# Rotary embedding over eight batches: the first small store takes two rows a partition in place of one

## The chip, the core and the metric

The kernel runs on one core of a Trainium2 chip. The metric is the device time of one execution in microseconds (us). Before the change the median of 3 runs is 317.09 us (316.78 to 317.14).

## The reference

The input x has 8 batches of 2048 positions, 16 heads and 64 values, in float32. Each head is split into two halves of 32 values, and each pair of values is turned by an angle that depends on the position:

```
cos = cos[None, :, None, :].copy()
sin = sin[None, :, None, :].copy()
out1 = x1 * cos - x2 * sin
out2 = x1 * sin + x2 * cos
return np.concatenate([out1, out2], axis=-1).astype(np.float32)
```

There are three operations for each value. 67.1 MB of x are read and as much is written.

## The kernel before

**Tiling.** The 2048 positions of a batch lie on 128 partitions, so a partition holds J = 16 consecutive positions, called rows here. A row is 16 heads of 64 values: 4 KB in DRAM (float32) and 2 KB on chip (float16). One tile `xt` holds a whole batch, 32 KB a partition. A pool of NBUF = 5 tiles serves the eight batches, so batch 5 takes over the tile of batch 0, batch 6 that of batch 1, and batch 7 that of batch 2.

**Transfers.** The loads (L52) and nearly all stores (L60, L100, L130, L132) are issued by GpSimd, which lets the transfer change the type on the way: a load turns float32 into float16, and a store turns it back. Three small transfers at the start are issued by SP: the first JA = 2 rows of batch 0 in float32 (`head`, L36), and the sine and cosine tables (L44, L45). ScalarE turns these into float16 (L84, L88 to L90). SP also sends the last two rows of batch 7 out (L141), after ScalarE has turned them into float32 in `head` (L140).

**Arithmetic.** `rotate` has three VectorE instructions: x with its halves swapped times the signed sine, into a scratch tile `v` (L73), x times the cosine in place (L79), and the sum of the two, again in place (L81). Batch 0 is rotated in two parts: rows 0 and 1 first, which need only the `head` rows, and then rows 2 to 15. Batches 1 to 7 are rotated whole.

**Order.** GpSimd issues its transfers in the order in which they stand in its program, and it waits before an issue until what the transfer needs is ready. The order is this: load 0 (rows 2 to 15), load 1, the small store of batch 0's row 0 (L100), loads 2, 3 and 4, the store of batch 0's rows 1 to 15, store 1, load 5, load 6, store 2, store 3, load 7, stores 4, 5 and 6, and batch 7 in pieces of 9 rows (`gate`, L130) and 5 rows (`rest`, L132). The place of the small store is set by hand: two ordering edges without a semaphore put it behind load 1 and ahead of load 2. Load 5 waits until batch 0 is stored, load 6 until batch 1 is, and load 7 until batch 2 is. SP's last store waits for `gate` to land.

Of the kernel before, what the change touches and what calls it, by code (L numbers as in the profile page):

```python
# [1 line left out]

# [4 lines left out]


@with_exitstack  # L10
def kernel(
    ctx: ExitStack,
    tc: tile.TileContext,
    x: bass.AP,
    cos: bass.AP,
    sin: bass.AP,
    out: bass.AP,
):
    nc = tc.nc
    f16 = mybir.dt.float16  # L20
    f32 = mybir.dt.float32

    B, S, H, D = x.shape
    Dh = D // 2
    P = nc.NUM_PARTITIONS
    J = S // P
    NBUF = 5

    const_pool = ctx.enter_context(tc.tile_pool(name="rope_const", bufs=1))
    io_pool = ctx.enter_context(tc.tile_pool(name="rope_io", bufs=NBUF))  # L30
    tmp_pool = ctx.enter_context(tc.tile_pool(name="rope_tmp", bufs=1))

    JA = 2
    head = const_pool.tile([P, JA, H, D], f32)
    x0 = x[0].rearrange("(p j) h d -> p j (h d)", j=J)
    nc.sync.dma_start(  # L36
        out=head.rearrange("p j h d -> p (j h d)"),
        in_=x0[:, 0:JA, :].rearrange("p j f -> p (j f)"),
    )
    sin_f = const_pool.tile([P, J, Dh], f32)  # L40
    cos_f = const_pool.tile([P, J, Dh], f32)
    cos_h = const_pool.tile([P, J, Dh], f16)
    sin_h = const_pool.tile([P, J, D], f16)
    nc.sync.dma_start(out=sin_f, in_=sin.rearrange("(p j) d -> p j d", j=J))  # L44
    nc.sync.dma_start(out=cos_f, in_=cos.rearrange("(p j) d -> p j d", j=J))  # L45

    loads = []

    def load(b):
        xt = io_pool.tile([P, J, H, D], f16)  # L50
        j0 = JA if b == 0 else 0
        dma = nc.gpsimd.dma_start(  # L52
            out=xt[:, j0:J, :, :].rearrange("p j h d -> p (j h d)"),
            in_=x[b].rearrange("(p j) h d -> p j (h d)", j=J)[:, j0:J, :].rearrange("p j f -> p (j f)"),
        )
        loads.append(dma)
        return xt

    def store(b, xt, j0=0):
        return nc.gpsimd.dma_start(  # L60
            out=out[b].rearrange("(p j) h d -> p j (h d)", j=J)[:, j0:J, :].rearrange("p j f -> p (j f)"),
            in_=xt[:, j0:J, :, :].rearrange("p j h d -> p (j h d)"),
        )

    def rotate(xt, j0, j1):
        v = tmp_pool.tile([P, J, H, D], f16)
        n = j1 - j0
        js = slice(j0, j1)
        shape = [P, n, H, 2, Dh]
        sin_b = sin_h[:, js, :].rearrange("p j (e d) -> p j e d", e=2).unsqueeze(2).to_broadcast(shape)  # L70
        cos_b = cos_h[:, js, :].unsqueeze(2).to_broadcast([P, n, 2 * H, Dh])
        xe = xt[:, js, :, :].rearrange("p j h (e d) -> p j h e d", e=2)
        nc.vector.tensor_mul(  # L73
            out=v[:, js, :, :].rearrange("p j h (e d) -> p j h e d", e=2),
            in0=xe[:, :, :, ::-1, :],
            in1=sin_b,
        )
        xw = xt[:, js, :, :].rearrange("p j h (e d) -> p j (h e) d", d=Dh)
        nc.vector.tensor_mul(out=xw, in0=xw, in1=cos_b)  # L79
        xa = xt[:, js, :, :].rearrange("p j h d -> p (j h d)")  # L80
        nc.vector.tensor_add(out=xa, in0=xa, in1=v[:, js, :, :].rearrange("p j h d -> p (j h d)"))  # L81

    tiles = [load(b) for b in range(2)]
    nc.scalar.copy(  # L84
        out=tiles[0][:, 0:JA, :, :].rearrange("p j h d -> p (j h d)"),
        in_=head.rearrange("p j h d -> p (j h d)"),
    )
    nc.scalar.copy(out=sin_h[:, :, Dh:D], in_=sin_f)  # L88
    nc.scalar.mul(out=sin_h[:, :, 0:Dh], in_=sin_f, mul=-1.0)  # L89
    nc.scalar.copy(out=cos_h, in_=cos_f)  # L90
    rotate(tiles[0], 0, JA)
    def part(b, j0, j1):
        return (
            out[b].rearrange("(p j) h d -> p j (h d)", j=J)[:, j0:j1, :].rearrange("p j f -> p (j f)"),
            tiles[b][:, j0:j1, :, :].rearrange("p j h d -> p (j h d)"),
        )

    def store_rows(b, j0, j1):
        dst, src = part(b, j0, j1)
        return nc.gpsimd.dma_start(out=dst, in_=src)  # L100

    first = store_rows(0, 0, 1)
    tc.add_manual_dep(
        first.ins,
        loads[1].ins.name,
        mybir.DependencyInfo(mybir.DependencyClass.NoSync, mybir.DependencyReason.DATA),
        reason="order of the ring",
    )
    tiles += [load(b) for b in range(2, NBUF)]
    tc.add_manual_dep(  # L110
        loads[2].ins,
        first.ins.name,
        mybir.DependencyInfo(mybir.DependencyClass.NoSync, mybir.DependencyReason.DATA),
        reason="order of the ring",
    )
    for b in range(B):
        rotate(tiles[b], JA if b == 0 else 0, J)
        if b < B - 1:
            st = store(b, tiles[b], 1 if b == 0 else 0)
            if b == 0:  # L120
                tc.add_manual_dep(
                    st.ins,
                    first.ins.name,
                    mybir.DependencyInfo(mybir.DependencyClass.NoSync, mybir.DependencyReason.DATA),
                    reason="order of the ring",
                )
        if b + NBUF < B:
            tiles.append(load(b + NBUF))
    dst, src = part(B - 1, 0, 9)
    gate = nc.gpsimd.dma_start(out=dst, in_=src)  # L130
    dst, src = part(B - 1, 9, J - JA)
    rest = nc.gpsimd.dma_start(out=dst, in_=src)  # L132
    tc.add_manual_dep(
        rest.ins,
        gate.ins.name,
        mybir.DependencyInfo(mybir.DependencyClass.NoSync, mybir.DependencyReason.DATA),
        reason="order of the ring",
    )
    dst, src = part(B - 1, J - JA, J)
    nc.scalar.copy(out=head.rearrange("p j h d -> p (j h d)"), in_=src)  # L140
    end = nc.sync.dma_start(out=dst, in_=head.rearrange("p j h d -> p (j h d)"))  # L141
    tc.add_manual_dep(
        end.ins,
        gate.ins.name,
        mybir.DependencyInfo(mybir.DependencyClass.Sync, mybir.DependencyReason.DATA),
        reason="the last rows go out behind this part",
    )


# [1 line left out]
_INS = ['x', 'cos', 'sin']  # L151
_OUTS = [((8, 2048, 16, 64), 'float32')]


# [23 lines left out]
```

## Time and profile before

| What | Value |
|---|---|
| Median of 3 runs | 317.09 us (316.78 to 317.14) |
| The profiled execution's own time | 316.67 us |
| Its span (first to last instruction) | 314.9 us |
| VectorE (DVE) busy | 209.1 us, 66% of the span, 27 instructions |
| ScalarE (ACT) busy | 6.8 us, 2% |
| GpSimd (POOL) busy | 9.9 us, 3% |
| TensorE | not used |
| Bytes moved by GpSimd's queue (q0) | 99.09 MB in 2592 packets, counted at the destination |
| Bytes moved by SP's queue (q1) | 2.62 MB in 576 packets |

The page gives busy time by engine, the span in 40 equal slices with a digit for the busy tenths, the queues of the transfers, and the costliest groups of instructions with what ended the idle time before them. Further views of the same trace list the instructions in order of time, who waited for whom, and each transfer's time from its issue to its landing. Bytes are counted where they land: a load counts its float16 bytes, a store its float32 bytes. Issuing a transfer is no busy time of the queue: what GpSimd spends on an issue (about 0.5 us) and what the transfer takes are two different numbers.

### The profile page before, as it was taken

What the parts mean: (1) busy time and instruction counts of PE and PEld (TensorE: products, weight loads), DVE (VectorE), ACT (ScalarE), POOL (GpSimd) and SP (SyncE); (2) the same over time, 40 slices, a digit from 0 to 9 for tenths busy, and PEclk for the clock granted to TensorE, in tenths of its full rate; (3) what the DMA queues carried; (4) which work ended last, traced back from release to release, by engine and by line L of the source; (5) the groups of instructions that cost most, each with busy time, mean ns of one, the idle gap of its engine ahead of it and who ended that gap; (6) DMA issues with size and microseconds to landing.
All of it is one profiled execution on the core that took longest, in us unless ns stands there. A gap on an engine that the chain in (4) does not pass through costs nothing.

```text
span 314.9 us, 122 instructions
## 1 busy us (share of the span) xinstructions
DVE 209.1 (66%) x27; ACT 6.8 (2%) x6; POOL 9.9 (3%) x22
## 2 busy tenths in 40 slices
DVE  0010699999999999999999999995009993000000
ACT  4100000000000000000000000000000002000000
POOL 1000200000000000010000000200000001000000
DMA  9899999999999899999999999999999999999997
GB/s 280 184 262 206 200 266 200 200 262 204 200 200 325 375 492 407 400 350 250 200 200 237 362 400 400 491 441 266 200 316 416 400 400 524 408 400 400 433 443 323
DMA packets 3168, 101.71 MB, mean 323 GB/s; under 512 B 352, under 2 KB 352, under 8 KB 736
## 3 DMA queue, kind: packets, MB, share of 16 engines
q0 software_dynamic: 2592, 99.09, 98.1%
q1 hardware_dynamic: 576, 2.62, 2.2%
HBM read 67.63 MB, written 67.11 MB: 428 GB/s over the span
## 4 chain that ended last, share of the span: by engine, by line
DVE 25%; DMA 22%; issue 18%; another core or an unknown queue 17%; ACT 1%; POOL 1%; SPq 0%; POOLq 0%; DVEq 0%; ACTq 0%
DMA xt<-in_x_dram 12%; DMA cos_f<-in_cos_dram 10%; DVE xt L81 8%; DVE xt L79 8%; DVE v L73 8%; ACT head L140 1%; POOL out_dram L60 0%; POOL xt L52 0%; ACT cos_h L90 0%; SPq L44 0%; SPq L36 0%; POOLq L52 0%; DVEq L73 0%; ACTq L140 0%
## 5 line engine op out<-in xcount | busy, mean ns | idle before, releaser
L73 DVE TENSOR_TENSOR v<-xt,sin_h 128x16384 f16<-128x16384 f16 (+2 forms) x9 | 69.7, 7744 | 36.0 <-DMA xt<-in_x_dram 20.0
L79 DVE TENSOR_TENSOR xt<-xt,cos_h 128x16384 f16<-128x16384 f16 (+2 forms) x9 | 69.7, 7744 | 17.4 <-ACT cos_h L90 17.2
L81 DVE TENSOR_TENSOR xt<-xt,v 128x16384 f16<-128x16384 f16 (+2 forms) x9 | 69.7, 7745 | 0.3
L52 POOL DMA_DIRECT2D xt<-in_x_dram x8 | 4.4, 556 | 110.4 <-DMA out_dram<-xt 109.6
L140 ACT CAST head<-xt 128x2048 f32<-128x2048 f16 x1 | 1.9, 1897 | 228.8 <-DVE xt L81 228.8
L60 POOL DMA_DIRECT2D out_dram<-xt x7 | 3.7, 535 | 63.6 <-DVE xt L81 63.6
L84 ACT CAST xt<-head 128x2048 f16<-128x2048 f32 x1 | 1.9, 1897 | 3.5 <-DMA head<-in_x_dram 3.5
L130 POOL DMA_DIRECT2D out_dram<-xt x1 | 0.5, 531 | 45.6 <-DVE xt L81 45.6
L100 POOL DMA_DIRECT2D out_dram<-xt x1 | 0.5, 536 | 34.5 <-DVE xt L81 34.5
L84 ACT ACT_TABLE_LOAD x1 | 1.3, 1283 | 0.7 <-PEq L162 0.7
L90 ACT CAST cos_h<-cos_f 128x512 f16<-128x512 f32 x1 | 0.6, 617 | 17.8 <-DMA cos_f<-in_cos_dram 17.8
L88 ACT CAST sin_h<-sin_f 128x512 f16<-128x512 f32 x1 | 0.6, 617 | 7.2 <-DMA sin_f<-in_sin_dram 7.2
L89 ACT ACTIVATE sin_h<-sin_f 128x512 f16<-128x512 f32 x1 | 0.6, 624 | 0.0
L132 POOL DMA_DIRECT2D out_dram<-xt x1 | 0.5, 531 | 0.0
L162 POOL MEMSET const-float32-0.0<- 128x1 f32 x1 | 0.1, 98 | 0.2 <-issue 0.2
L162 POOL MEMSET const-bfloat16-1.0<- 128x1 bf16 x1 | 0.1, 101 | 0.0
L162 POOL MEMSET const-float32-1.0<- 128x1 f32 x1 | 0.1, 98 | 0.0
L162 POOL MEMSET const-uint8-127<- 128x1 uint8 x1 | 0.1, 98 | 0.0
## 6 DMA issues: line engine op xcount, KB each, us to landing
xt<-in_x_dram POOLq DMA_DIRECT2D x7, 4096.0 KB, 38.3
out_dram<-xt POOLq DMA_DIRECT2D x1, 7680.0 KB, 60.9
out_dram<-xt POOLq DMA_DIRECT2D x1, 4608.0 KB, 42.4
xt<-in_x_dram POOLq DMA_DIRECT2D x1, 3584.0 KB, 22.3
out_dram<-xt POOLq DMA_DIRECT2D x1, 2560.0 KB, 47.9
head<-in_x_dram SPq DMA_DIRECT2D x1, 1024.0 KB, 4.8
out_dram<-head SPq DMA_DIRECT2D x1, 1024.0 KB, 8.4
out_dram<-xt POOLq DMA_DIRECT2D x1, 512.0 KB, 7.8
```

Source lines behind the costliest of these rows:

```text
L52: dma = nc.gpsimd.dma_start(out=xt[:, j0:J, :, :].rearrange("p j h d -> p (j h d)"), in_=x[b].rearrange("(p j) h d -> p j (h d)", j=J)[:, ...
L60: return nc.gpsimd.dma_start(out=out[b].rearrange("(p j) h d -> p j (h d)", j=J)[:, j0:J, :].rearrange("p j f -> p (j f)"), in_=xt[:, j0:J ...
L73: nc.vector.tensor_mul(out=v[:, js, :, :].rearrange("p j h (e d) -> p j h e d", e=2), in0=xe[:, :, :, ::-1, :], in1=sin_b,)
L79: nc.vector.tensor_mul(out=xw, in0=xw, in1=cos_b)
L81: nc.vector.tensor_add(out=xa, in0=xa, in1=v[:, js, :, :].rearrange("p j h d -> p (j h d)"))
L84: nc.scalar.copy(out=tiles[0][:, 0:JA, :, :].rearrange("p j h d -> p (j h d)"), in_=head.rearrange("p j h d -> p (j h d)"),)
L88: nc.scalar.copy(out=sin_h[:, :, Dh:D], in_=sin_f)
L89: nc.scalar.mul(out=sin_h[:, :, 0:Dh], in_=sin_f, mul=-1.0)
L90: nc.scalar.copy(out=cos_h, in_=cos_f)
L100: return nc.gpsimd.dma_start(out=dst, in_=src)
L130: gate = nc.gpsimd.dma_start(out=dst, in_=src)
L140: nc.scalar.copy(out=head.rearrange("p j h d -> p (j h d)"), in_=src)
```

## The change

The small store of batch 0 covers rows 0 and 1 (8 KB a partition) in place of row 0 alone (4 KB). The store of the rest of batch 0 covers rows 2 to 15 in place of 1 to 15. The order of the transfers is now written as a list (`plan`): "L" is a load, "R" a rotation, "S" a store, each with its batch and its rows. Each transfer that GpSimd issues has an ordering edge without a semaphore to the one before it, where there were four such edges at single places before. The branch "L4" is used by no entry of the list. The core of the diff:

```diff
-    first = store_rows(0, 0, 1)
-    tc.add_manual_dep(
-        first.ins,
-        loads[1].ins.name,
-        mybir.DependencyInfo(mybir.DependencyClass.NoSync, mybir.DependencyReason.DATA),
-        reason="order of the ring",
-    )
-    tiles += [load(b) for b in range(2, NBUF)]
...
-    for b in range(B):
-        rotate(tiles[b], JA if b == 0 else 0, J)
-        if b < B - 1:
-            st = store(b, tiles[b], 1 if b == 0 else 0)
...
-        if b + NBUF < B:
-            tiles.append(load(b + NBUF))
...
+    plan = (
+        ("L", 0, 2, 16),
+        ("L", 1, 0, 16),
+        ("R", 0, 0, 2),
+        ("S", 0, 0, 2),
+        ("L", 2, 0, 16),
+        ("L", 3, 0, 16),
+        ("L", 4, 0, 16),
+        ("R", 0, 2, 16),
+        ("S", 0, 2, 16),
+        ("R", 1, 0, 16),
+        ("S", 1, 0, 16),
+        ("L", 5, 0, 16),
+        ("L", 6, 0, 16),
+        ("R", 2, 0, 16),
+        ("S", 2, 0, 16),
+        ("R", 3, 0, 16),
+        ("S", 3, 0, 16),
+        ("L", 7, 0, 16),
...
+    def ring(out, in_, **kw):
+        nonlocal last
+        dma = nc.gpsimd.dma_start(out=out, in_=in_, **kw)
+        if last is not None:
+            behind(dma, last, mybir.DependencyClass.NoSync)
+        last = dma
+        return dma
...
+    for what, b, j0, j1 in plan:
+        if what == "L":
+            if b not in tiles:
+                tiles[b] = io_pool.tile([P, J, H, D], f16, name="xt")
+            ring(held(b, j0, j1), rows(x, b, j0, j1))
+        elif what == "L4":
+            ring(held(b, j0, j1), rows(x, b, j0, j1), max_dma_last_dim=4096)
+        elif what == "S":
+            ring(rows(out, b, j0, j1), held(b, j0, j1))
+        else:
+            rotate(b, j0, j1)
+    gate = ring(rows(out, B - 1, 0, 9), held(B - 1, 0, 9))
+    ring(rows(out, B - 1, 9, J - JA), held(B - 1, 9, J - JA))
+    nc.scalar.copy(out=flat, in_=held(B - 1, J - JA, J))
+    end = nc.sync.dma_start(out=rows(out, B - 1, J - JA, J), in_=flat)
+    behind(end, gate, mybir.DependencyClass.Sync)
```

## The prediction

> **What bounds the kernel now.** I read the page from its second part, the span in 40 slices, because no engine is busy for more than 66% of it and something else has to set the end. Slices are 314.9 / 40 = 7.87 us wide; the digits are tenths.
>
> ```profile
> DVE  0010699999999999999999999995009993000000
> ...
> DMA  9899999999999899999999999999999999999997
> ...
> HBM read 67.63 MB, written 67.11 MB: 428 GB/s over the span
> ```
>
> The reader is to see that VectorE has holes (at the start, near 220 us, after 263 us) and the transfers have none: nearly every digit is 9, two are 8, and the last is 7 because the span ends behind it. The bytes are fixed by the problem: every input is read once and every output is written once. At 134.74 MB in 314.9 us, only idle or slowed transfer time can be won or lost.
>
> Next I wanted each transfer's share of that time. GpSimd issues all the large transfers. The timeline says when each is issued, and the view of the DMA issues, narrowed to one issue at a time, says how long it took until it landed. First the timeline around the change (start, duration, engine, line):
>
> ```profile
> 36.95 0.54 POOL L100 DMA_DIRECT2D out_dram<-xt  x1 [34.49 <-DVE xt L81]
> 37.47 1.59 POOL L52 DMA_DIRECT2D xt<-in_x_dram  x3
> ...
> 59.92 0.54 POOL L60 DMA_DIRECT2D out_dram<-xt  x1 [20.86 <-DVE xt L81]
> ...
> 85.84 8.69 DVE L73 TENSOR_TENSOR v<-xt,sin_h 128x16384 f16<-128x16384 f16 x1
> 86.11 0.54 POOL L60 DMA_DIRECT2D out_dram<-xt  x1 [25.64 <-DVE xt L81]
> ```
>
> and the page's list of issues (the last number is us from issue to landing; KB are counted at the destination, so a load of 16 rows is 4,096 KB and a store of 16 rows 8,192 KB):
>
> ```profile
> out_dram<-xt POOLq DMA_DIRECT2D x1, 7680.0 KB, 60.9
> out_dram<-xt POOLq DMA_DIRECT2D x1, 4608.0 KB, 42.4
> ...
> out_dram<-xt POOLq DMA_DIRECT2D x1, 2560.0 KB, 47.9
> ...
> out_dram<-xt POOLq DMA_DIRECT2D x1, 512.0 KB, 7.8
> ```
>
> Issue plus this time is the landing. The small store (512 KB) lands at 36.95 + 7.8 = 44.75; the store of the other 15 rows of batch 0 (7,680 KB) at 59.92 + 60.9 = 120.8. The same view asked for single issues gives load 1 at 43.4, load 2 at 64.0, load 3 at 83.3, load 4 at 102.6, store 1 at 86.11 + 54.0 = 140.1, load 5 at 159.4, load 6 at 178.8, store 2 at 198.1, store 3 at 217.4, load 7 at 236.7, stores 4, 5 and 6 at 256.0, 275.3 and 294.7, and the three pieces of batch 7 at 305.6 (9 rows), 311.6 (5 rows) and 314.0 (2 rows, SP's queue). The reader is to see that they land one behind the other in the order of issue, and that the distance between two landings goes by bytes alone. A full load or store takes 19.2 to 19.4 each time, 1.21 us a row. The 15 rows took 120.8 - 102.6 = 18.2 (1.21 a row), the 9 rows 10.9 (1.21), the 5 rows 6.0 (1.20) and the one row of the small store 44.75 - 43.4 = 1.35. So from 2 us to 311.6 GpSimd's queue is one gapless belt, and what bounds the kernel is its length.
>
> Last the waits, to see whether the belt is ever short of work:
>
> ```profile
> POOL xt L52 <- DMA out_dram<-xt: 109.6, 3, 56.1
> ...
> DVE v L73 <- DMA xt<-in_x_dram: 20.0, 1, 20.0
> ...
> ACT cos_h L90 <- DMA cos_f<-in_cos_dram: 17.8, 1, 17.8
> ```
>
> GpSimd waits (load 5 for store 0, load 6 for store 1, load 7 for store 2) while the next transfer, 19.3 us of it, already lies on the belt. The 20.0 us are VectorE waiting for load 7 at 236.7; behind that load stores 4, 5 and 6 keep the belt going until 294.7, and batch 7 is ready to be issued at 263.17. No wait starves the belt.
>
> **The change part by part.** The listing of the two programs' instructions, engine by engine, has the same number, order and waits on all of them. Two instructions differ in size: the small store goes from 128x1024 to 128x2048 elements, and batch 0's other store from 128x15360 to 128x14336. The list that now drives the order, the helper functions and the ordering edges between all transfers without a semaphore add no instruction and no wait: cost 0.
>
> *The small store, one row more.* It is released by the addition of rows 0 and 1 (L81, ending at 36.65), which already covered both rows, so the second row waits for nothing new. Issue takes 0.54 us; nearby issues of 4,096 KB to 8,192 KB take 0.53 to 0.54 too, so the size adds nothing on GpSimd. Loads 2, 3 and 4, queued behind it on GpSimd, are issued at 37.47 as now. The belt is then still busy with load 1 until 43.4, 5.9 us of cover. On the belt the row adds 1.21 us. The trace shows no two-row store on this queue, so I bound it: 1.20 a row (the 5-row piece) gives 2.40 in all, and twice the one-row slot gives 2.70. I take 1.35 + 1.21 = 2.56, which is nearest to the many rows at 1.21, and keep -0.15 to +0.15 for the range.
>
> *Loads 2, 3 and 4, moved.* They land 1.21 later: at 65.2, 84.5 and 103.8. VectorE takes up batch 2 at 85.84, batch 3 at 112.03 and batch 4 at 138.21. Even the tightest has 20.6 us of cover left. Were it gone, VectorE would be late by up to 1.21, and the stores behind it with it.
>
> *The rest store of batch 0, one row less.* Its slot shrinks from 18.2 to 18.2 - 1.21 = 17.0. It starts 1.21 later and lands at 103.8 + 17.0 = 120.8, as now. So loads 5, 6 and 7 are released when they are now, and the end with them. What it waits for on VectorE (the end of batch 0's addition at 59.64) stands.
>
> *Sum:* +1.21 - 1.21 = 0 on the belt, 0 elsewhere. From the profiled execution, 316.67 + 0 = 316.67 us (its span is 314.9; 1.8 lie around it). The runs shown have a median of 317.09, 0.42 above that execution, and lie between 316.78 and 317.14. The median plus 0 is the forecast: 317.1.
>
> One rule speaks for the change. The row: the 512 KB store took 1.35 us of the belt where one row's bytes cost 1.21, so its smallness cost 0.14. The Trainium skill, "DMA: Bandwidth & Descriptors", section "Bandwidth", asks for batches of at least 1 MiB, exactly what the small store becomes, and its section "Anatomy of one DMA" fits a transfer at about 2.0 us plus its bytes at 436 GB/s. By that fit the lone 512 KB would take an estimated 3.2 us; the trace's 1.35 disagrees, as the queue's neighbours cover nearly all of the fixed part. Were the 2.0 us exposed and cured at 1 MiB, the sum would be an estimated 314.7 in place of 316.67.
>
> **The rivals.** *Slower: load 2 arrives too late.* Place: VectorE's first multiplication of batch 2. Price: the 1.21 us by which the loads shift, if the lateness is passed on to stores 2 and 3 and the belt stands still for it; 317.1 + 1.2 = 318.3. It decides only from the point where load 2 lands behind 85.84; it lands at 64.0. For it: load 7 shows that VectorE can wait for a load (20.0 us). Against it: 20.6 us of cover, and those 20.0 us cost nothing. Chance 0.05, which also takes in a transfer of two rows that disturbs its neighbours in a way that no row of this trace shows.
>
> *Faster: the small store's slot is a fixed cost, not one of bytes.* Then two rows take 1.35 as well, the rest store still loses 1.21, and the belt ends earlier by it: 317.1 - 1.2 = 315.9. For it: 1.35 is the one slot above the line. Against it: the 5- and 9-row pieces show no fixed part, and two rows in 1.35 would be 1,024 KB at 777 GB/s, where a full store's distance of 19.3 gives 435. Chance 0.04.
>
> *The change does nothing that can be timed because it is not what it says:* excluded as a case of its own. The instruction listing shows the two sizes, and its time would be the forecast's.
>
> **How the numbers follow.** The forecast, no change, has 0.87. The two rivals have 0.05 and 0.04, and 0.04 is left for causes I don't see, half to each side. A measurement of this kernel can tell about 0.2% from no change, which is 0.63 us; both rivals lie beyond it, and the forecast's bounds of 0.15 within it. So faster is 0.04 + 0.02 = 0.06, slower 0.05 + 0.02 = 0.07, same 0.87. The range has to leave out no more than 2 in 10, and the forecast alone holds more than 8. Its low end is the profiled execution less 0.15 and some scatter, 316.4. Its high end is the slowest run, 317.14, plus 0.15 and the 0.36 by which the runs differ, 317.7.
>
> **What would show it.** In the profile of the changed kernel: an issue of 1,024 KB that lands near 46.0 (about 9.0 after its issue), the loads behind it 1.2 later, an issue of 7,168 KB that lands at 120.8 again (60.9 after an issue at 59.9), and load 5 issued at 121.4. The DMA digits stay as they are, and VectorE's groups keep their means (7,744 ns). The step "the belt's length is a sum of bytes" is wrong if batch 0's rest store lands more than 0.3 from 120.8; the step "the delay of loads 2 to 4 is hidden" is wrong if VectorE idles before batch 2, 3 or 4. The prediction as a whole is wrong if either shift is still there at the landing of load 7 (236.7).

## The result and the profile after

The changed kernel has a median of 317.44 us (317.23 to 317.84, 15 runs), the kernel before 316.84 us in the same comparison (316.56 to 317.21, 15 runs). The ratio is 1.0017 with a 95% interval of 1.001 to 1.0023. That is inside the forecast's range (316.4 to 317.7) and inside 0.2%, but no change (a ratio of 1) lies outside the interval: the kernel became some 0.6 us slower, where the sum said 0. The ratios here are estimates from all runs of a comparison and need not be the ratio of the two medians, which is 1.0019 in this case. The profiled execution takes 317.56 us; its span is 315.8 us, 0.9 longer than before.

The slices of the page show the same picture as before, nearly every digit of the transfers a 9 (the 8 in the middle has moved by one slice, which means little: no_small_store below is as slow and has a 9 in both places):

```profile
DMA  9899999999999989999999999999999999999997
...
HBM read 67.63 MB, written 67.11 MB: 427 GB/s over the span
```

The timeline of GpSimd's issues (start, duration, engine, line) and then the page's list of issues (KB at the destination, us from issue to landing):

```profile
37.03 0.54 POOL L95 DMA_DIRECT2D out_dram<-xt  x1 [34.58 <-DVE xt L118]
37.56 1.59 POOL L95 DMA_DIRECT2D xt<-in_x_dram  x3
...
60.01 0.54 POOL L95 DMA_DIRECT2D out_dram<-xt  x1 [20.85 <-DVE xt L118]
...
85.92 8.69 DVE L110 TENSOR_TENSOR v<-xt,sin_h 128x16384 f16<-128x16384 f16 x1
86.19 0.54 POOL L95 DMA_DIRECT2D out_dram<-xt  x1 [25.64 <-DVE xt L118]
...
122.28 0.53 POOL L95 DMA_DIRECT2D xt<-in_x_dram  x1 [35.56 <-DMA out_dram<-xt]
```

```profile
out_dram<-xt POOLq DMA_DIRECT2D x1, 7168.0 KB, 61.7
...
out_dram<-xt POOLq DMA_DIRECT2D x1, 1024.0 KB, 9.8
```

The small store lands at 37.03 + 9.8 = 46.8 (46.0 was said), batch 0's other store at 60.01 + 61.7 = 121.7 (120.8 was said), and load 5 is issued at 122.28 (121.4 was said). All of them are late by the same 0.8 to 0.9. So the time isn't lost between the small store and the end of batch 0. It is lost ahead of the small store, which the landing of load 1 shows. The view of the issues narrowed to load 1, first before, then after:

```profile
xt<-in_x_dram POOLq DMA_DIRECT2D x1, 4096.0 KB, 41.5
```

```profile
xt<-in_x_dram POOLq DMA_DIRECT2D x1, 4096.0 KB, 42.4
```

Load 1 was issued at the same time in both and took 0.9 us longer, though nothing about it was changed. The reader is to see how a cost can fall on the transfer ahead of the one that was edited.

The trace also records each packet of a transfer. A full load has 128 packets, one for each partition. The records don't name the DMA engine. But 128 packets of 2.43 us in 19.3 us are 16 at a time, so I take eight for each of the 16 engines, and the 16 packets that start last as the last one on each. A packet of a full load takes 2.43 us in both kernels, within 0.02 or so. Only the last packets of load 1, the load directly ahead of the small store, are clearly longer: 2.66 us on average before and 3.46 after. Below, the *stretch* is this mean over the 16 last packets less 2.43: 0.23 us before and 1.03 after, 0.80 apart. About 0.1 of the span's 0.9 remains; in this profile the `head` rows, which the change doesn't touch, already land 0.1 later. From the small store's first packet on, every distance on the queue is the predicted one (the two rows 2.45 us where 2.56 was said, the 14 rows 16.9 where 17.0 was said; between first packets the one row of before took 1.25 and the 15 rows 18.1, so the row did move from one slot to the other at 1.2 us).

### The profile page after: what moved, and what is told of

Same layout as the page of the kernel before. It is cut to its first block, busy times and chain, and to the rows that moved or that the text cites. A ratio compares the mean times of both kernels' runs of the same rounds, so it can differ in the third digit from the quotient of the medians.

```text
span 315.8 us, 122 instructions
## 1 busy us (share of the span) xinstructions
DVE 209.1 (66%) x27; ACT 6.8 (2%) x6; POOL 9.9 (3%) x22
## 4 chain that ended last, share of the span: by engine, by line
DVE 25%; DMA 22%; issue 18%; another core or an unknown queue 17%; ACT 1%; POOL 1%; SPq 0%; POOLq 0%; DVEq 0%; ACTq 0%
DMA xt<-in_x_dram 12%; DMA cos_f<-in_cos_dram 10%; DVE xt L118 8%; DVE xt L116 8%; DVE v L110 8%; ACT head L140 1%; POOL out_dram L95 0%; POOL xt L95 0%; ACT cos_h L125 0%; SPq L44 0%; SPq L36 0%; POOLq L95 0%; DVEq L110 0%; ACTq L140 0%
## 5 line engine op out<-in xcount | busy, mean ns | idle before, releaser
L110 DVE TENSOR_TENSOR v<-xt,sin_h 128x16384 f16<-128x16384 f16 (+2 forms) x9 | 69.7, 7744 | 37.0 <-DMA xt<-in_x_dram 20.8
## 6 DMA issues: line engine op xcount, KB each, us to landing
out_dram<-xt POOLq DMA_DIRECT2D x1, 7168.0 KB, 61.7
out_dram<-xt POOLq DMA_DIRECT2D x1, 4608.0 KB, 42.4
```

The lines of the kernel that those rows point to most:

```text
L110: nc.vector.tensor_mul(out=v[:, js, :, :].rearrange("p j h (e d) -> p j h e d", e=2), in0=xe[:, :, :, ::-1, :], in1=sin_b,)
```

## The experiments

The expectations name theories by letters. A: a store of two rows directly behind a load stretches that load's end. B: the rewriting of the order costs the time. C: the small store reaches a queue that is nearly empty. D: the first store of a run pays, once and less if it is small, and frees the later ones. E: the stretch is paid once, at the first change from loads to a store, and its size goes by the bytes of the store there. F: of these it is the bytes read on chip that count. G: the bytes written early count. S: chance. The experiments were made in three comparisons, each with its own runs of the kernel before: medians 317.37 us (one_row_list to two_one_row), 316.88 (tiny_gp to half_row) and 317.05 (after_again to f32_row).

| Run | Store directly behind load 1 (or another), bytes a partition on chip | Stretch, us | Ratio to before (95%) |
|---|---|---|---|
| before | 2 KB | 0.23 at load 1, 0.02 at load 4 | 1 |
| after | 4 KB | 1.03 at load 1 | 1.0017 (1.001 to 1.0023) |
| after, again | 4 KB | 0.97 at load 1 | 1.003 (1.0021 to 1.0039) |
| one_row_list | 2 KB | 0.37 at load 1 | 1.0004 (0.9994 to 1.0014) |
| no_small_store | none; 32 KB behind load 4 | 0.99 at load 4 | 1.0015 (1.0006 to 1.0023) |
| behind_load2 | 4 KB, behind load 2 | 1.04 at load 2 | 1.002 (1.0009 to 1.0031) |
| two_one_row | 2 KB and 2 KB | 1.13 at load 1 | 1.0025 (1.0016 to 1.0034) |
| tiny_gp | 0.5 KB behind load 0, 4 KB behind load 1 | 0.82 at load 1 | 1.0023 (1.0014 to 1.0032) |
| tiny_gp_no_small | 0.5 KB behind load 0, 32 KB behind load 4 | 0.76 at load 4 | 1.0018 (1.0009 to 1.0026) |
| tiny_sp | 4 KB behind load 1, after a gap | 0 at load 1, 0.89 at load 4 | 1.0139 (1.0124 to 1.0153) |
| half_row | 1 KB; 31 KB behind load 4 | 0.02 at load 1, 0.61 at load 4 | 1.0004 (0.9995 to 1.0014) |
| split_rows | 2 KB, and 2 KB behind load 2 | 0.55 at load 1, 0 at loads 2 and 4 | 1.0007 (0.9998 to 1.0017) |
| ladder | 1 KB, 1 KB, 2 KB behind loads 1, 2, 3 | 0.07 at load 1, 0 at 2, 3 and 4 | 0.9983 (0.9974 to 0.9992) |
| f32_row | 4 KB (4 KB in DRAM) | 0.84 at load 1 | 1.006 (1.0046 to 1.0073), with one row more to write |

Where a load isn't named, its stretch is 0.03 or less. The stretches are of one profiled execution each; the ratios are of all runs. The profiled executions of half_row and behind_load2 were the slowest of their runs (319.33 us beside a median of 317.14, and 318.49 beside 317.9). The stretch is a mean over 16 engines, and the landing waits for the slowest of them.

**one_row_list: only the rewriting is left.**

```diff
-        ("S", 0, 0, 2),
+        ("S", 0, 0, 1),
...
-        ("S", 0, 2, 16),
+        ("S", 0, 1, 16),
```

> The changed kernel with the small store set back to one row (and the rest store to 15 rows): only the rewriting of the order as a list is left of the change. Theory A (the second row of the small store stretches the last packets of load 1, the belt's last work ahead of it, by some 0.8 us more than one row does): 316.8, ratio to before 1.000, load 1 lands about 41.5 after its issue. Theory B (the rewriting costs the time, by its ordering edges or another layout): 317.4, ratio 1.0017, load 1 lands about 42.4 after its issue.

Measured: 317.33 beside 317.37, ratio 1.0004 (0.9994 to 1.0014). Theory B's 1.0017 lies outside the interval and B falls; no cost of the list and its ordering edges shows. The stretch is 0.37, which also shows how much one profile of the one-row store differs from another. The landing of load 1 doesn't part the two theories: 42.1 after its issue, between A's 41.5 and B's 42.4.

**no_small_store: nothing behind load 1.**

```diff
-        ("S", 0, 0, 2),
...
-        ("S", 0, 2, 16),
+        ("S", 0, 0, 16),
```

> The changed kernel without the small store: batch 0 is stored whole behind load 4, and loads 2 to 4 are issued at the start. Theory A: no store follows load 1, so its last packets are not stretched at all (2.43 us each, as the others), and the time is about 0.25 below before, 316.6 (ratio 0.999). Theory B: 317.4. Theory C (the stretch comes from new work reaching the queue when it holds only load 1's last packets): also 316.6, since loads 2 to 4 are queued early.

Measured: ratio 1.0015 (1.0006 to 1.0023), slower, against theories A and C. B's number would fit, but B has fallen with one_row_list. The view of the issues, narrowed to loads 1, 2, 3 and 4, which are issued one behind the other, about 0.5 us apart:

```profile
xt<-in_x_dram POOLq DMA_DIRECT2D x1, 4096.0 KB, 41.1
...
xt<-in_x_dram POOLq DMA_DIRECT2D x1, 4096.0 KB, 59.9
...
xt<-in_x_dram POOLq DMA_DIRECT2D x1, 4096.0 KB, 78.8
...
xt<-in_x_dram POOLq DMA_DIRECT2D x1, 4096.0 KB, 98.8
```

With 0.5 between issues, loads 2 and 3 land 19.3 and 19.4 after the load ahead of them, load 4 20.5. The missing us has moved to load 4, the load that now has the first store behind it. So the cost isn't tied to the small store; it came here at the first change from loads to a store, and with one row there it was smaller (0.23 to 0.55).

**behind_load2: the store elsewhere, and queued early.**

```diff
-        ("S", 0, 0, 2),
         ("L", 2, 0, 16),
+        ("S", 0, 0, 2),
```

> The two-row store behind load 2 in place of load 1: the same neighbours (a full load ahead, a full load behind), but load 2 is issued at the start, so the store and the loads behind it reach the queue some 25 us before their turn, not 6. Theory A (the neighbourhood of a load and a small store makes the stretch, wherever it is): the last packets of load 2 take about 3.4 us in place of 2.43 and the time stays at 317.4 (ratio 1.002). Theory C (late arrival in a short queue): no stretch at load 1 or load 2, 316.6 (ratio 0.999).

Measured: ratio 1.002 (1.0009 to 1.0031), stretch 1.04 at load 2 and none at load 1. The store was issued at 34.4 and its first packet started at 62.7, so it didn't come late: theory C falls.

**two_one_row: the same bytes in two transfers.**

```diff
-        ("S", 0, 0, 2),
+        ("S", 0, 0, 1),
+        ("S", 0, 1, 2),
```

> Rows 0 and 1 go out in two small stores of one row each, one behind the other, in place of one of two rows: as many bytes, packets half as large and twice as many. Theory A in the form 'it goes by the size of a packet (4 KB against 8 KB)': stretch of about 0.25 as with one row, 316.9 (ratio 1.000). Theory A in the form 'it goes by the bytes of the small store': stretch of about 1.0, 317.4 (ratio 1.0017). Theory C says nothing on the size; the issue of one more transfer (0.53 us) shifts loads 2 to 4 by 0.5 in a queue that is busy until 43.

Measured: ratio 1.0025 (1.0016 to 1.0034), stretch 1.13. So halving the packets and the transfers didn't lessen it; what lies directly behind the load in the queue counts, over the border of two transfers.

**tiny_gp: a first store of 0.5 KB ahead of it.**

```diff
         ("L", 0, 2, 16),
+        ("W", 0, 0, 1),
...
+    warm = const_pool.tile([P, 256], f16)
+    nc.vector.memset(warm, 0.0)
...
+        elif what == "W":
+            tiny = ring(rows(out, 0, 0, 1)[:, 0:256], warm)
         elif what == "S":
-            ring(rows(out, b, j0, j1), held(b, j0, j1))
+            dma = ring(rows(out, b, j0, j1), held(b, j0, j1))
+            if b == 0 and j0 == 0:
+                behind(dma, tiny, mybir.DependencyClass.Sync)
```

> The changed kernel with one more transfer: a store of 1 KB a partition (zeros, written over by the small store later) on GpSimd's queue between load 0 and load 1. The four runs before showed a stretch of about 1 us in the last load packets ahead of the first store of the run, wherever that store was, and none ahead of any later one. Theory D (the first store of the run costs it once, less where that store is small): the tiny store takes it, at most some 0.3 us in load 0's last packets, load 1's last packets take 2.43 us in spite of the two-row store behind them, and the time falls to about before or slightly above: tiny store 0.3 + first-row cost 0.3, so 316.9 to 317.2 where before is 316.8 (ratio 1.000 to 1.001). Theory A (any two-row store behind a load makes it): load 1's last packets still take about 3.4 us, ratio 1.002 to 1.003.

Measured: ratio 1.0023 (1.0014 to 1.0032), stretch 0.82 at load 1. The tiny store held the queue for 0.48 us itself. (Of the four runs that the expectation looks back on, one_row_list had 0.37, not about 1.) Theory D falls as it was put: a tiny first store doesn't free the others. It went with 0.2 less stretch; the one-row store's three profiles differ by more than that (0.23, 0.37 and 0.55).

**tiny_gp_no_small: the same ahead of a whole batch.** It has the tiny store's edit and leaves out the small store as above.

> The same tiny store of 1 KB a partition between load 0 and load 1 and no small store at all; batch 0 goes out whole behind load 4. Theory D: no stretch of 1 us ahead of batch 0's store, ratio to the kernel without the small store 0.998, to before about 1.000. Theory A': (the first full-size store behind a load stretches, whatever came before): load 4's last packets take about 3.4 us as without the tiny store, ratio 1.0015 to 1.002.

Measured: ratio 1.0018 (1.0009 to 1.0026), stretch 0.76 at load 4. It agrees with the run before: 0.23 less than without the tiny store (0.99).

**tiny_sp: the tiny store on SP's queue.**

```diff
+    tiny = nc.sync.dma_start(out=rows(out, 0, 0, 1)[:, 0:256], in_=flat[:, 0:256])
...
-            ring(rows(out, b, j0, j1), held(b, j0, j1))
+            dma = ring(rows(out, b, j0, j1), held(b, j0, j1))
+            if b == 0 and j0 == 0:
+                behind(dma, tiny, mybir.DependencyClass.Sync)
```

> The changed kernel with the tiny store of 1 KB a partition issued by SP on its own queue (from the rows in head, behind the cosine table; written over later), so that DRAM's output has been written once before GpSimd's queue carries its first store. Theory D1 (the cost belongs to the first write of the output memory by the core): no stretch of load 1's last packets, ratio about 1.000. Theory D2 (it belongs to the first store of GpSimd's queue): the stretch of 1.0 us stays, ratio 1.002.

Measured: ratio 1.0139 (1.0124 to 1.0153); neither expectation. The edit brought a stall that I had not reckoned with, by the semaphore edge that makes the small store wait for the tiny one, and it is in the waits:

```profile
POOL out_dram L95 <- DMA out_dram<-head: 41.7, 1, 41.7
```

The tiny store landed late, GpSimd waited for it, and the small store was issued only at 44.17. GpSimd's queue ran empty for about 2 us. The run therefore doesn't test load 1 as it was meant to. But the trace shows that the two-row store, behind a gap, stretched nothing, and that a stretch of 0.89 came at the next change, from load 4 to 14 rows. By then the output had been written from SP's queue and from GpSimd's, so this 0.89 belongs neither to the first write of the output (D1) nor to the first store of GpSimd's queue (D2).

**half_row: half a row.**

```diff
-        ("S", 0, 0, 2),
+        ("H", 0, 0, 1),
...
-        ("S", 0, 2, 16),
+        ("T", 0, 0, 16),
...
+        elif what == "H":
+            ring(rows(out, b, 0, 1)[:, 0:512], held(b, 0, 1)[:, 0:512])
+        elif what == "T":
+            ring(rows(out, b, 0, 16)[:, 512:16384], held(b, 0, 16)[:, 512:16384])
```

> The small store covers half a row (2 KB a partition) in place of two rows, the rest store 15.5 rows. Stretch of the last load packets ahead of the small store: it was 0.2 to 0.4 us with one row, 1.0 with two rows and with sixteen. If it goes by the bytes of the first store, up to a ceiling of 1 us, half a row gives 0.1 to 0.2; if a floor of about 0.25 comes with any store, 0.25. Another possibility: the part that the small first store does not take is then taken by the rest store behind load 4 (0.06 us on 4 packets in the kernel before), 0.8 us there. Time about 316.7 to 316.9 beside 316.84 (ratio 0.9995 to 1.000); with the last possibility 317.4.

Measured: ratio 1.0004 (0.9995 to 1.0014), stretch 0.02 at load 1 and 0.61 at load 4. The stretches are those of the last possibility: what a small first step doesn't take, the next one does. The time is not: 317.4 would be a ratio of 1.0018, outside the interval. The stretch comes from the slowest of the 11 runs, 319.33, in which the first packets of load 2 already start 1.73 us apart (0.50 before), so this run speaks for the last possibility and doesn't settle it.

**after_again.** The changed kernel, unedited.

> The changed kernel once more, for a second profile and for a comparison on the same chip as the three others: 317.4, ratio 1.0017, and load 1's last packets about 1.0 us above 2.43 if the stretch belongs to the kernel; if it was chance in one profile (theory S), anything from 0 to 1.0.

Measured: ratio 1.003 (1.0021 to 1.0039), stretch 0.97. Theory S falls for the two-row store. The whole interval lies above 1.002 here.

**split_rows: never two rows together.**

```diff
-        ("S", 0, 0, 2),
+        ("S", 0, 0, 1),
         ("L", 2, 0, 16),
+        ("S", 0, 1, 2),
```

> Row 0 goes out behind load 1 as before, row 1 by itself behind load 2: the same bytes as the changed kernel's small store, but never two rows together. Theory E (the stretch is paid once, at the first change from loads to a store, and its size goes by the bytes that follow in a row there): 0.25 to 0.4 us at load 1, 0 at load 2 and load 4, ratio to before 1.000 and to the changed kernel 0.998. Theory A (each change pays by what follows it): 0.25 to 0.4 at load 1 and again at load 2, ratio 1.001. Theory G (it goes by all bytes written early): 1.0 in all, ratio 1.0017.

Measured: ratio 1.0007 (0.9998 to 1.0017), on the same chip as the changed kernel's 1.003, whose interval lies above. Stretch 0.55 at load 1, more than in the other profiles of one row, and none at load 2 or load 4: theory E, against A and G. The ratio itself doesn't part E's 1.000 from A's 1.001; the missing stretch at load 2 does.

**ladder: three steps.**

```diff
-        ("S", 0, 0, 2),
+        ("H", 0, 0, 512),
         ("L", 2, 0, 16),
+        ("H", 0, 512, 1024),
         ("L", 3, 0, 16),
+        ("S", 0, 1, 2),
...
+        elif what == "H":
+            ring(rows(out, b, 0, 1)[:, j0:j1], held(b, 0, 1)[:, j0:j1])
```

> The two rows in three steps: half a row behind load 1, the other half behind load 2, row 1 behind load 3, and 14 rows behind load 4. Half a row alone gave 0.07 at load 1 and left 0.6 for the rest store behind load 4. If a later, larger step pays only what earlier ones haven't (theory E with steps): 0.07 at load 1, less than 0.3 at loads 2 and 3 together, none at load 4, sum below 0.4, time at or up to 0.2 below before (ratio 0.9995 to 1.000). If half rows leave the sum as it is: 0.6 to 0.7 in all, ratio 1.001.

Measured: 316.83 beside 317.05, ratio 0.9983 (0.9974 to 0.9992). It is below both kernels: slightly below the kernel before (the medians alone give 0.9993), and clearly below the changed kernel, which stood at 1.003 on the same chip. The stretch at load 1 is the 0.07 that was expected; half_row itself showed 0.02 there, not the 0.07 that the expectation quotes. The timeline around batch 0, and behind it load 5 of the kernel before:

```profile
36.73 0.54 POOL L97 DMA_DIRECT2D out_dram<-xt  x1 [34.28 <-DVE xt L120]
37.25 0.54 POOL L97 DMA_DIRECT2D xt<-in_x_dram  x1
37.77 0.54 POOL L97 DMA_DIRECT2D out_dram<-xt  x1
38.30 0.55 POOL L97 DMA_DIRECT2D xt<-in_x_dram  x1
38.82 0.56 POOL L97 DMA_DIRECT2D out_dram<-xt  x1
39.34 0.56 POOL L97 DMA_DIRECT2D xt<-in_x_dram  x1
...
121.26 0.54 POOL L97 DMA_DIRECT2D xt<-in_x_dram  x1 [34.84 <-DMA out_dram<-xt]
```

```profile
121.38 0.53 POOL L52 DMA_DIRECT2D xt<-in_x_dram  x1 [34.74 <-DMA out_dram<-xt]
```

Load 5 is issued at 121.26, 1.02 ahead of the changed kernel (122.28) and 0.12 ahead of the kernel before, though GpSimd issues two transfers more than the changed kernel and the same two rows go out early.

**f32_row: bytes on chip against bytes in DRAM.**

```diff
-        ("S", 0, 0, 2),
+        ("F", 0, 0, 1),
...
-        ("S", 0, 2, 16),
+        ("S", 0, 0, 16),
...
+        elif what == "F":
+            early = ring(rows(out, 0, 0, 1), flat[:, 0:1024])
         elif what == "S":
-            ring(rows(out, b, j0, j1), held(b, j0, j1))
+            dma = ring(rows(out, b, j0, j1), held(b, j0, j1))
+            if b == 0 and j0 == 0:
+                behind(dma, early, mybir.DependencyClass.Sync)
```

> The small store takes one row in float32 from head (the rows as loaded, written over by the rest store, which covers all 16 rows here): 4 KB a partition on chip as the two float16 rows have, 4 KB in DRAM as the one row has; it is queued early, behind load 1. One row more is on the belt (1.21 us), so the time by itself is compared less that. If the stretch goes by the bytes read on chip (theory F): 1.0 us at load 1, none at load 4; if by the bytes written to DRAM: 0.25 to 0.4 at load 1. Time 316.84 + 1.2 = 318.0 by the latter (ratio 1.004), 318.7 by the former (ratio 1.006).

Measured: 319.02 beside 317.05, ratio 1.006 (1.0046 to 1.0073), stretch 0.84. With the same 4 KB in DRAM as the one row (0.23, 0.37 and 0.55) and the same 4 KB on chip as the two rows (1.03 and 0.97), it lies nearer to the latter, and the ratio is F's. The run changes more than the bytes (the source tile, that no type is changed on the way, and that the store is queued at 5.6 us), so it speaks for F and doesn't settle it.

## Why the prediction was right, and what its sum lacked

*What bounds the kernel* held. GpSimd's queue ran without a gap in both kernels (from its first packet at 5.1 us; the prediction said 2), and every distance from the small store on was the bytes' own: 2.45 for the two rows, 16.9 for the 14, 19.3 for each full transfer.

*The small store, one row more.* Its own slot was right. The step that failed is the term it left at nothing: "On the belt the row adds 1.21 us", and no more. The row also lengthened the end of load 1, by 0.80 us in the two profiles. In the sum this is +0.8 where 0 stood, and the medians moved by 0.60. The prediction bounded the new store's slot to 0.15 on both sides and put no bound on what it does to its neighbour. That the time still fell inside the range was in part luck: the room above 317.1 had been left for scatter between runs, not for this term, and in the repeat (after_again) the ratio was 1.003 and the median 317.94, above the range, where the kernel before had 317.05.

*The trace of before had the sign.* The prediction's own numbers give load 0's landing at 1.25 + 22.3 = 23.55 and load 1's at 43.4, 19.85 apart, where the later loads are 19.2 to 19.4 apart. I read the list of landings from load 1 on and passed over it. 0.23 of this half us is the stretch. Some 0.1 is there without any store behind load 1 (no_small_store shows 19.45 between the first packets of loads 1 and 2), probably from the cosine table's packets, which run until 30.7. The rest I can't account for.

*Loads 2, 3 and 4, moved,* were hidden as forecast. Load 2 landed at 37.56 + 28.5 = 66.1, VectorE took up batch 2 at 85.92 without waiting. Its only wait for a load is the old one, now 20.8 us long, since load 7 is late by the same 0.9:

```profile
POOL xt L95 <- DMA out_dram<-xt: 110.4, 3, 56.1
...
DVE v L110 <- DMA xt<-in_x_dram: 20.8, 1, 20.8
```

*The rest store, one row less,* shrank as said. Its landing failed the mark that the prediction had set (more than 0.3 from 120.8), through no doing of its own: it began late. The mark for the prediction as a whole failed too: a shift was still there when load 7 landed. VectorE takes it up 0.9 later, here before and after:

```profile
236.73 8.69 DVE L73 TENSOR_TENSOR v<-xt,sin_h 128x16384 f16<-128x16384 f16 x1 [20.02 <-DMA xt<-in_x_dram]
...
237.62 8.69 DVE L110 TENSOR_TENSOR v<-xt,sin_h 128x16384 f16<-128x16384 f16 x1 [20.83 <-DMA xt<-in_x_dram]
```

*The rivals.* Load 2 never came too late. The one direction that the prediction gave a share without a price, "a transfer of two rows that disturbs its neighbours in a way that no row of this trace shows", was the one that came, at half to two thirds of the rival's 1.2 us; and a row did show it, load 1's distance above. The faster rival is refuted by the slot of 2.45.

*The rule of at least 1 MiB a transfer*, which the prediction took from the Trainium skill ("DMA: Bandwidth & Descriptors", section "Bandwidth"), would have made this change a gain. In this queue, which never ran empty, the runs show no such gain: with the transfer of 1 MiB the kernel was slower than with the 512 KB one, two transfers of 512 KB behind one another were no better (1.0025), and the ladder's smaller ones cost less.

*What is shown and what is not.* Shown: the lost time of the changed kernel lies in the last load packets ahead of a store; it came at the first such change of a run and, after a step of one row or more had been made without a gap, at no later one; it grows with what lies behind the load (0.02 to 0.07 us for 1 KB a partition, 0.23 to 0.55 for 2 KB, 0.97 to 1.13 for two rows in one or two transfers, 0.99 for 32 KB). Shown by one run each: three small steps avoid nearly all of it (ladder), and after an empty queue it had to be paid at the next change (tiny_sp). Not shown is the mechanism. That the engines fetch ahead what lies behind the load, and hold back the load's own last data for it, is a guess; no run looks inside a packet, and why it happens only once stays open. Open, too, is whether bytes on chip alone decide, and why one row gave 0.23, 0.37 and 0.55 in three profiles.

## What to carry to other kernels

When a queue of transfers is the bound, make the sum over its landings from the very first one, and ask of each distance that is off the line which neighbour it stands next to; an edit can lengthen the transfer ahead of it. If a kernel loads for a while before it first stores, a few small stores of growing size between the loads can make the change cheaper than one larger one: here 1, 1 and 2 KB a partition gave 0.9983 where 4 KB at once gave 1.003, in one comparison. A term taken as 0 because bytes are only moved from one transfer to another needs a bound on the neighbours as well.

## What the runs showed of the hardware that I had not expected

The first change from loads to a store on GpSimd's queue cost up to 1.13 us in the mean of the last load packets (two_one_row, all 16 of them between 3.44 and 3.81 us in place of 2.43), and it did so with every byte ready and queued 40 us ahead (no_small_store: 0.99, issued at 59.7, its turn at 101.4). Later changes of the same kind, once a row or more had gone out without a gap, cost 0.03 us or less. In tiny_sp the wait of GpSimd for a tiny transfer on SP's queue left its own queue empty for about 2 us: the tiny transfer's packets came behind the cosine table's, took turns with load 1's, and the last one ended at 43.15 us, just behind load 1's last at 43.01.
